# Where the rotary tables and the splits of weight units 4 and 5 stand in the first stage of a decoder trunk

## The chip, the cores and the metric

The kernel runs on one core of a Trainium2 chip. The metric is device time in microseconds of one execution, the median of several runs; lower is better. One further execution was profiled, and all lines of the profile are from it.

## The reference

Two decoder layers over 256 tokens of width 1024, in float32. What matters here is the start of the first layer:

```python
cos, sin = rope_tables(positions)           # angles: position x inverse frequency
h = rmsnorm(x, attn_norm[l])
q, k, v = jnp.split(h @ w_qkv_a[l], 3, axis=-1)
q = partial_rope(heads(q, N_HEADS), cos, sin)   # the first 16 of each head's 64 dims
k = partial_rope(heads(k, N_HEADS), cos, sin)
o = moba_attention(to_bhsd(q), to_bhsd(k), to_bhsd(heads(v, N_HEADS)))
```

With 256 tokens and a block of 256, this attention is plain causal attention of 16 heads. Then follow its output projection, a gated feed-forward layer with a causal convolution, a second layer of sliding-window attention with shared keys and values and a second feed-forward layer, and a last norm.

## The kernel before, in words

**Units and splits.** All weights are packed into units of 128 x 2048 values. Unit i is fetched by SyncE into the raw tile `wr` of that number (three buffers in rotation, so unit i + 3 waits for the last read of unit i). Each value is then split into a high part `wh`, rounded to TensorE's fp32r type, and a low part `wl`, the rest; the activations are split the same way, and a product is three matmuls (high x high, high x low, low x high), accumulated in PSUM. `hi_part` (L163) makes the high part on ScalarE, `lo_part` (L166) the low part on VectorE. `wh` and `wl` have four buffers each. A unit is split in quarters of 512 columns or halves of 1024.

**The first stage.** Units 0 and 1 are the first half of V's weights, which arrive chunk by chunk together with x (`first_parts`, `v_first`); units 2 and 3 are the weights of Q and K of head group 0, units 4 and 5 of group 1, 6 and 7 of group 2, 8 and 9 the second half of V, 10 and 11 of group 3. TensorE computes the first V half, then `qk_group(0)`: for each 128 rows of weights, three matmuls into each of two accumulators (K's and Q's, column half 0), then column half 1 of K's and of Q's. `rotate_f` (L418) reads such an accumulator on VectorE in four instructions (a shuffle, two products with the tables, a sum), ScalarE makes the high part (L432), VectorE the low part (L437), and GpSimd copies K's parts into the block-diagonal tile `kd` (L952). `scores` then multiplies Q and K of a group, and the softmax of its four heads runs on VectorE (L514, L535, L542) and ScalarE (L524, L540), while TensorE works on the next groups from a generator of filling work; `attention` gets a lead of 8000 (ns of counted TensorE work) between the end of group 0 and the first scores. After the softmax TensorE turns the probabilities (L555) and multiplies them by V (L578).

**The row norm and the tables.** The norm's factor per token is not applied to x but later, to the accumulated products. `square` (ScalarE, L301) sums the squares of a row block's halves, `rstd_of` takes two small VectorE instructions (L308, L309) and a GpSimd power (L310). V is scaled by it in `v_out` (L840). For Q and K the factor is folded into the rotary tables: `tables` makes sine and cosine (VectorE L917, GpSimd L918, ScalarE L919, GpSimd L922 and L923), `new_tables` spreads them over 64 dims on GpSimd (L390 to L394), scales them per row block on ScalarE (L400), has TensorE turn them (L406, four transposes) and ScalarE copy the result out (L411). `rotate_f` cannot run before that.

**What sets the order.** In this first stage PE, ScalarE, VectorE and SyncE run in the order in which the code issues (`manual`); GpSimd's and everything behind the stage is ordered by a scheduler. The order of issuing comes from deferred chains: `chain` puts a step off to a time on a counted clock, `tick` advances that clock by the work of each matmul and runs what is due, `require` forces a step. `first_norm` is put off to 3000 and `tables_a` to 3010 on that clock; `used(0)` and `used(1)` put the splits of units 4 and 5 off, four quarters each, with a fetch of unit i + 3 at the end of unit i.

## Time and profile before

| | us |
|---|---|
| median of 3 runs | 569.88 |
| lowest, highest | 569.54, 570.95 |
| the profiled execution | 569.15 |
| its span, first to last instruction | 567.4 |
| mean granted TensorE clock | 0.991 |

A timeline row gives start and length in microseconds, engine, line, operation, the tiles written and read, their shapes and the count of instructions merged; in brackets stands the idle time of the engine just before it and what ended it. A row of waits gives the total, the number of times and the longest. A windows row gives a stretch, its length, then each engine's busy time (PE, PEld, VectorE, ScalarE, GpSimd) with its number of instructions, the granted clock (PEclk), the share of the DMA engines and GB/s. An issues row ends in the microseconds from issue to landing. DVE is VectorE, ACT ScalarE, POOL GpSimd, SPq SyncE's queue. Times count from the start of the span.

### The profile page before, as it was taken

To read this page: it belongs to the slowest core of one execution; us is meant where nothing else is said; L and a number is where in the kernel's file an instruction comes from. 1 tells how busy PE (TensorE), PEld (TensorE's weight loads), DVE (VectorE), ACT (ScalarE), POOL (GpSimd) and SP (SyncE) were. 2 spreads that over 40 slices of the span, in tenths; PEclk is the share of its full clock that TensorE was granted. 3 is DMA by queue.
4 is the path that set the end of the run, shared out by engine and by line. 5 is a ranking of instruction groups with operands and counts; after the bars stand their busy time and mean duration, and the time that the engine had idled before them with its cause. 6 is when DMAs were issued, how large, how long until landed. Compare 5 with 4: busy or idle time off the path is not lost.

```text
span 567.4 us, 10530 instructions
## 1 busy us (share of the span) xinstructions
PE 550.1 (97%) x4022; PEld 512.6 (90%) x4022; DVE 437.0 (77%) x928; ACT 379.0 (67%) x771; POOL 104.0 (18%) x130
## 2 busy tenths in 40 slices
PE   8789999999999999999999999999999999999995
PEld 7679989889999999988887988889999999998884
DVE  6589988788899888864449989878988888874414
ACT  6846887887567777753439788887666777763413
POOL 7221102002232233110000100001432233210003
PEclk9889999999999999999999999999999999999998
DMA  8834472533384666555561832333265566666301
GB/s 321 361 120 178 153 243 77 206 139 103 122 288 160 222 223 223 200 198 202 217 219 43 268 137 96 129 98 126 102 219 206 218 223 223 213 210 222 135 0 74
DMA packets 15312, 101.00 MB, mean 178 GB/s; under 512 B 1952, under 2 KB 2080, under 8 KB 3744
## 3 DMA queue, kind: packets, MB, share of 16 engines
q1 hardware_dynamic: 14976, 100.09, 49.6%
q8 instruction: 31, 0.51, 0.3%
q10 hardware_dynamic: 288, 0.26, 0.1%
q14 instruction: 17, 0.14, 0.1%
HBM read 99.30 MB, written 1.05 MB: 177 GB/s over the span
## 4 chain that ended last, share of the span: by engine, by line
PE 84%; DVE 7%; ACT 4%; DMA 2%; issue 1%; POOL 1%; SPq 0%; DVEq 0%; POOLq 0%; ACTq 0%
PE acc L628 9%; PE acc L629 9%; PE acc L633 9%; PE u L725 6%; PE u L724 6%; PE u L723 6%; PE t L725 6%; PE t L724 6%; PE t L723 6%; DVE wl L167 3%; PE acc L452 2%; PE acc L454 2%; PE acc L453 2%; PE acc L724 2%; PE acc L723 2%; PE acc L725 2%
## 5 line engine op out<-in xcount | busy, mean ns | idle before, releaser
L167 DVE TENSOR_TENSOR wl<-wr,wh 128x1024 fp32r<-128x1024 f32 (+1 forms) x208 | 222.6, 1087 | 64.8 <-ACT wh L164 63.5
L164 ACT ACTIVATE wh<-wr 128x1024 fp32r<-128x1024 f32 (+1 forms) x208 | 189.4, 944 | 63.3 <-PE acc L633 51.7
L767 POOL TENSOR_TENSOR m<-m,m 128x256 f32<-128x256 f32 x44 | 64.7, 1470 | 176.2 <-DVE m L762 111.1
L628 PE MATMUL acc<-wh,q 128*128 128x512 f32 x238 | 92.0, 386 | 0.0
L629 PE MATMUL acc<-wl,q 128*128 128x512 f32 x238 | 90.6, 380 | 0.0
L723 PE MATMUL u<-q,wh 128*128 128x256 f32 x320 | 88.4, 277 | 0.0
L724 PE MATMUL u<-q,wh 128*128 128x256 f32 x320 | 88.2, 276 | 0.0
L725 PE MATMUL u<-q,wl 128*128 128x256 f32 x320 | 88.0, 275 | 0.0
L725 PE MATMUL t<-q,wl 128*128 128x256 f32 x288 | 79.2, 275 | 0.0
L723 PE MATMUL t<-q,wh 128*128 128x256 f32 x288 | 79.2, 275 | 0.0
L724 PE MATMUL t<-q,wh 128*128 128x256 f32 x288 | 79.2, 275 | 0.0
L633 PE MATMUL acc<-wh,q 128*128 128x512 f32 x238 | 74.6, 379 | 0.0
L724 PEld LDWEIGHTS u<-q,wh 128*128 128x128 f32 x320 | 60.1, 188 | 0.0
L725 PEld LDWEIGHTS u<-q,wl 128*128 128x128 f32 x320 | 60.1, 188 | 0.0
L723 PEld LDWEIGHTS u<-q,wh 128*128 128x128 f32 x320 | 59.9, 188 | 0.0
L723 PEld LDWEIGHTS t<-q,wh 128*128 128x128 f32 x288 | 54.1, 188 | 0.0
L724 PEld LDWEIGHTS t<-q,wh 128*128 128x128 f32 x288 | 54.1, 188 | 0.0
L725 PEld LDWEIGHTS t<-q,wl 128*128 128x128 f32 x288 | 54.1, 188 | 0.0
L628 PEld LDWEIGHTS acc<-wh,q 128*128 128x128 f32 x238 | 45.0, 189 | 7.0 <-issue 0.9
L633 PEld LDWEIGHTS acc<-wh,q 128*128 128x128 f32 x238 | 45.0, 189 | 6.3
L629 PEld LDWEIGHTS acc<-wl,q 128*128 128x128 f32 x238 | 45.0, 189 | 5.9 <-issue 0.2
L771 ACT ACTIVATE q<-m 128x256 fp32r<-128x256 f32 x44 | 18.1, 416 | 40.0 <-POOL m L767 40.0
(187 smaller groups left out, 1129.4 us busy)
## 6 DMA issues: line engine op xcount, KB each, us to landing
wr<-in_w SPq DMA_DIRECT2D x90, 1024.0 KB, 4.8
first<-in_xw SPq DMA_DIRECT2D x5, 384.0 KB, 5.9
xr<-in_x SPq DMA_DIRECT2D x2, 512.0 KB, 8.2
first<-in_xw SPq DMA_DIRECT2D x1, 768.0 KB, 7.3
fin_t<-in_fin SPq DMA_DIRECT2D x1, 512.0 KB, 5.7
out<-ot SPq DMA_DIRECT2D x1, 512.0 KB, 2.6
first<-in_xw SPq DMA_DIRECT2D x1, 388.0 KB, 3.6
out<-m ACTq DMA_DIRECT2D x1, 256.0 KB, 2.1
```

Of the source, the lines that this page charges most:

```text
L164: nc.scalar.activation(wq[i][0][:, c], raws[i][:, c], AF.Copy)
L167: nc.vector.tensor_tensor(out=wq[i][1][:, c], in0=raws[i][:, c], in1=f(wq[i][0][:, c]), op=ALU.subtract)
L452: nc.tensor.matmul(om, wh, xh, start=(c == 0), stop=False)
L453: nc.tensor.matmul(om, wh, xl, start=False, stop=False)
L628: nc.tensor.matmul(pairs(o), ph[:, blk(b)], turns(hi[:, s_]), start=first, stop=False)
L629: nc.tensor.matmul(pairs(o), ph[:, blk(b)], turns(lo[:, s_]), start=False, stop=False)
L633: nc.tensor.matmul(pairs(o), pl[:, blk(b)], turns(hi[:, s_]), start=False, stop=end)
L723: nc.tensor.matmul(o, hi[:, s_], xh, start=(c == 0), stop=False)
L724: nc.tensor.matmul(o, hi[:, s_], xl, start=False, stop=False)
L725: nc.tensor.matmul(o, lo[:, s_], xh, start=False, stop=(c == KC - 1))
L767: nc.gpsimd.tensor_tensor(out=h, in0=gs, in1=t[1], op=ALU.mult)
L771: (3400.0, lambda: nc.scalar.activation(hi, h, AF.Copy)),
```

## The change

It does four things. The sine, its tables and their spreading are issued between the second and the third quarter of unit 3's splits. Unit 4 is split by VectorE alone: it makes the high part with a cast (`both_parts`) and the low part as before, and the squares and row statistics stand between its quarters; then the tables are scaled and V copied out. Unit 5's four quarters follow at once, on ScalarE and VectorE, with the fetches of units 7 and 8 beside them. The transposes of the tables are put off to 7700 on the counted clock, and the lead ahead of the first scores is 9000 instead of 8000. The deferred chains of units 4 and 5 are gone; later units start from a time of 8500.

```diff
     tab = [None]
+    TURN = 7700.0
-    def new_tables(rs_, key, *wait):
-        ex = mid().rearrange("p (b k e d) -> p b k e d", b=NB, k=2, e=2)
-        nc.gpsimd.memset(ex[:, :, 0, :, ROT:], 1.0)
-        nc.gpsimd.memset(ex[:, :, 1, :, ROT:], 0.0)
-        for k, t in enumerate((cs, sn)):
-            for e in range(2):
-                nc.gpsimd.tensor_copy(ex[:, :, k, e, :ROT], t)
+    def new_tables(rs_, key, between):
+        ex = tab[0]
         sc = mid().rearrange("p (b k f) -> p b k f", b=NB, k=2)
         new = quad(F32, "tab")[:, :2]
-        def scale():
-            for b in range(NB):
-                nc.scalar.activation(sc[:, b], ex[:, b].rearrange("p k e d -> p k (e d)"), AF.Copy, scale=rs_[b])
+        for b in range(NB):
+            nc.scalar.activation(sc[:, b], ex[:, b].rearrange("p k e d -> p k (e d)"), AF.Copy, scale=rs_[b])
+            between(b)
...
-        chain(key, *wait, (0.0, scale), (1200.0, turn))
+        chain(key, (TURN, turn))
...
-    for j in range(4):
-        part(3, slice(j * 512, (j + 1) * 512))
-    fetch(6)
-    nc.sync.dma_start(cp, cpk)
...
     def tables():
...
+        ex = mid().rearrange("p (b k e d) -> p b k e d", b=NB, k=2, e=2)
...
+        tab[0] = ex
+
+    for j in range(4):
+        part(3, slice(j * 512, (j + 1) * 512))
+        if j == 1:
+            tables()
+    fetch(6)
+    nc.sync.dma_start(cp, cpk)
...
     v_first(KC - 1)
-    def first_norm():
-        for b in range(NB):
-            for n in range(2):
-                square(b, n)
-            rs.append(rstd_of(b))
-        for b in range(NB):
-            v_out(b, 0, v_acc[b])
-    chain(("rs",), (3000.0, first_norm))
-    def tables_a():
-        tables()
-        new_tables(rs, ("rt",))
-    chain(("rt",), (3010.0, tables_a))
-    used(0)
-    used(1)
+    def quarter(k):
+        return slice(k * 512, (k + 1) * 512)
+    def both_parts(i, k):
+        nc.vector.tensor_copy(wq[i][0][:, quarter(k)], raws[i][:, quarter(k)])
+        lo_part(i, quarter(k))
+    weights(4)
+    weights(5)
+    for b in range(NB):
+        for n in range(2):
+            square(b, n)
+        both_parts(4, b)
+        rs.append(rstd_of(b))
+    new_tables(rs, ("rt",), lambda b: (v_out(b, 0, v_acc[b]), both_parts(4, 2 + b)))
+    fetch(7)
+    for k in range(4):
+        part(5, quarter(k))
+    fetch(8)
+    w_time[0] = 8500.0
...
-    attention(qk, ready_a, filler_a(), 8000.0, lambda g: (7000.0, 3500.0, 2000.0) if g < 3 else (4500.0, 2000.0, 1500.0), mask, lambda h: h, False)
+    attention(qk, ready_a, filler_a(), 9000.0, lambda g: (7000.0, 3500.0, 2000.0) if g < 3 else (4500.0, 2000.0, 1500.0), mask, lambda h: h, False)
```

In the rows of the order, `wh4_288` is the high part of unit 4, `wr4` its raw tile; numbers behind the underscore differ between the two programs. ScalarE, from unit 3 to the copy of the turned tables, before:

```order
L164 ACTIVATE wh3_253<-wr3_200 128x512 x4
L301 ACTIVATE m2_15_316,st_14_315<-xr0_92 128x512
L301 ACTIVATE m2_16_318,st_14_315<-xr0_92 128x512
L301 ACTIVATE m2_19_325,st_18_324<-xr1_93 128x512
L301 ACTIVATE m2_20_327,st_18_324<-xr1_93 128x512
L840 ACTIVATE v0_101<-acc_7_113,rstd_17_320 128x512
L840 ACTIVATE v1_102<-acc_8_114,rstd_21_329 128x512
L919 ACTIVATE rb_94<-rb_94 128x32
L400 ACTIVATE m2_23_349<-m2_22_342,rstd_17_320 128x256
L400 ACTIVATE m2_23_349<-m2_22_342,rstd_21_329 128x256
L164 ACTIVATE wh4_359<-wr4_238 128x512 x2
L411 ACTIVATE tab_24_350<-t_25_369 128x512
```

The same place on ScalarE now, where the sine is the instruction that writes `rb` and the tables' scaling the one that writes `m2_19`:

```order
L164 ACTIVATE wh3_253<-wr3_200 128x512 x2
L911 ACTIVATE rb_94<-rb_94 128x32
L164 ACTIVATE wh3_253<-wr3_200 128x512 x2
L301 ACTIVATE m2_12_293,st_11_292<-xr0_92 128x512
L301 ACTIVATE m2_13_295,st_11_292<-xr0_92 128x512
L301 ACTIVATE m2_16_304,st_15_303<-xr1_93 128x512
L301 ACTIVATE m2_17_306,st_15_303<-xr1_93 128x512
L395 ACTIVATE m2_19_314<-m2_10_268,rstd_14_299 128x256
L836 ACTIVATE v0_101<-acc_7_113,rstd_14_299 128x512
L395 ACTIVATE m2_19_314<-m2_10_268,rstd_18_310 128x256
L836 ACTIVATE v1_102<-acc_8_114,rstd_18_310 128x512
L164 ACTIVATE wh5_290<-wr5_251 128x512 x4
```

The sine has moved ahead of four squares and two V copies, the scaling stands ahead of each V copy, and unit 4 is gone from this engine.

VectorE from unit 3's splits to the first rotation's neighbourhood, before:

```order
L167 TENSOR_TENSOR wl3_254<-wr3_200,wh3_253 128x512 x4
L308 TENSOR_TENSOR st_14_315<-st_14_315 128x1
L309 TENSOR_SCALAR st_14_315<-st_14_315 128x1
L308 TENSOR_TENSOR st_18_324<-st_18_324 128x1
L309 TENSOR_SCALAR st_18_324<-st_18_324 128x1
L917 SCALAR_TENSOR_TENSOR rb_94<-rb_94 128x16
L167 TENSOR_TENSOR wl4_360<-wr4_238,wh4_359 128x512 x3
```

The same place on VectorE now, up to the second row block's statistics (two more casts and splits of unit 4 and the four splits of unit 5 follow):

```order
L167 TENSOR_TENSOR wl3_254<-wr3_200,wh3_253 128x512 x2
L909 SCALAR_TENSOR_TENSOR rb_94<-rb_94 128x16
L167 TENSOR_TENSOR wl3_254<-wr3_200,wh3_253 128x512 x2
L941 CAST wh4_288<-wr4_238 128x512
L167 TENSOR_TENSOR wl4_289<-wr4_238,wh4_288 128x512
L308 TENSOR_TENSOR st_11_292<-st_11_292 128x1
L309 TENSOR_SCALAR st_11_292<-st_11_292 128x1
L941 CAST wh4_288<-wr4_238 128x512
L167 TENSOR_TENSOR wl4_289<-wr4_238,wh4_288 128x512
L308 TENSOR_TENSOR st_15_303<-st_15_303 128x1
L309 TENSOR_SCALAR st_15_303<-st_15_303 128x1
```

The row statistics stand behind casts of unit 4 now, where they stood directly behind unit 3.

VectorE around unit 7 and the first mask steps of the softmax (`ISA`), before, from unit 7's first half on (the four instructions that write `m2_35` and `m2_34` are a rotation):

```order
L167 TENSOR_TENSOR wl7_551<-wr7_423,wh7_550 128x1024
L426 STREAM_SHUFFLE m2_35_527<-acc_32_453 128x512
L427 TENSOR_TENSOR m2_34_526<-acc_32_453,tab_24_350 128x512
L428 TENSOR_TENSOR m2_35_527<-m2_35_527,tab_24_350 128x512
L429 TENSOR_TENSOR m2_34_526<-m2_34_526,m2_35_527 128x512
L167 TENSOR_TENSOR wl6_493<-wr6_263,wh6_492 128x1024
L167 TENSOR_TENSOR wl7_551<-wr7_423,wh7_550 128x1024
L514 ISA m3_39_594,hst_41_596<-acc_36_569,mask_274 128x128
```

The same place on VectorE now, from that rotation to unit 7's second half:

```order
L422 STREAM_SHUFFLE m2_35_530<-acc_32_459 128x512
L423 TENSOR_TENSOR m2_34_529<-acc_32_459,tab_20_315 128x512
L424 TENSOR_TENSOR m2_35_530<-m2_35_530,tab_20_315 128x512
L425 TENSOR_TENSOR m2_34_529<-m2_34_529,m2_35_530 128x512
L167 TENSOR_TENSOR wl7_542<-wr7_324,wh7_541 128x1024
L510 ISA m3_39_615,hst_41_617<-acc_36_588,mask_336 128x128
L510 ISA hst_41_617 128x1
L433 TENSOR_TENSOR q_31_458<-m2_34_529,q_30_457 128x512
L510 ISA m3_40_616,hst_41_617<-acc_36_588,mask_336 128x128
L510 ISA hst_41_617 128x1
L167 TENSOR_TENSOR wl8_613<-wr8_334,wh8_612 128x1024
L167 TENSOR_TENSOR wl7_542<-wr7_324,wh7_541 128x1024
```

Unit 6 is done ahead of the rotation, and between the two halves of unit 7 stand two mask steps, a low part and half of unit 8. On TensorE 87 matmuls of units 4 and 5 stand ahead of the first scores, where 75 stood, and the four transposes of the tables stand behind 33 more matmuls of units 2 and 3.

## The prediction

> **What bounds the kernel now.** I read the page's head first, then the list of waits of TensorE.

> ```profile
> span 567.4 us, 10530 instructions
> PE 550.1 (97%) x4022; PEld 512.6 (90%) x4022; DVE 437.0 (77%) x928; ACT 379.0 (67%) x771; POOL 104.0 (18%) x130
> PE t L406 <- ACT m L400: 4.1, 1, 4.1
> PE acc L454 <- DVE wl L167: 2.5, 1, 2.5
> ```

> TensorE is the bound. Its two longest waits, the only ones above 2 us, lie in the stretch that the change rewrites. Its timeline there, with two windows of granted clock (column PEclk, third from the end):

> ```profile
> 21.00 0.28 PE L454 MATMUL acc<-q,wl 128*128 128x256 f32 x1
> 25.42 1.12 PE L406 MATMUL t<-ident,m 128*128 128x128 f32 x4 [4.14 <-ACT m L400]
> 26.18 0.56 PE L452 MATMUL acc<-q,wh 128*128 128x256 f32 x1
> 28.74 0.28 PE L452 MATMUL acc<-q,wh 128*128 128x256 f32 x1
> 30.89 0.28 PE L453 MATMUL acc<-q,wh 128*128 128x256 f32 x1
> 38.83 0.58 PE L454 MATMUL acc<-q,wl 128*128 128x256 f32 x1 [2.54 <-DVE wl L167]
> 42.32 0.29 PE L452 MATMUL acc<-q,wh 128*128 128x256 f32 x1
> 27.00:28.00 1.00, 1.00 (x6) 1.00 (x6) 0.77 (x3) 1.00 (x3) 0.00 (x0) 0.50 0.32 127
> 40.00:42.00 2.00, 2.00 (x12) 2.00 (x11) 2.00 (x3) 1.68 (x2) 1.90 (x2) 0.50 0.71 201
> ```

> Each wait is paid twice: the gap itself, then about 3.4 us of work at clock 0.50. At full clock a 256-column matmul starts every 0.113 us (19 steps from 28.74 to 30.89); I use 0.114.

> **What goes.** Gap one, 4.14. After it, 4 transposes and 12 matmuls fill 25.42 to 28.74, 3.32 us; at 0.114 a step they would take about 1.8, so 1.5 goes with it. Gap two, 2.54. After it 16 matmuls fill 38.83 to 42.32, 3.49 us against 1.82, so 1.67 goes. Together 9.85 us. What the chip gives of this depends on what is late next; I walk the new order with old durations.

> **Sine among unit 3's quarters.** The splits and the sine's steps as they stand now:

> ```profile
> 15.04 5.00 DVE L167 TENSOR_TENSOR wl<-wr,wh 128x512 fp32r<-128x512 f32 x8 [0.35 <-ACT wh L164]
> 16.88 2.20 ACT L164 ACTIVATE wh<-wr 128x512 fp32r<-128x512 f32 x4 [0.30 <-DMA wr<-in_w]
> 21.82 0.17 DVE L917 SCALAR_TENSOR_TENSOR rb<-rb 128x16 f32<-128x16 f32 x1
> 22.63 0.20 POOL L918 TENSOR_SCALAR rb<-rb 128x16 f32<-128x16 f32 x1
> 23.16 0.22 ACT L919 ACTIVATE rb<-rb 128x32 f32<-128x32 f32 x1
> ```

> VectorE's eight quarters step by 0.60, so the second of unit 3 ends at 20.04 - 1.2 = 18.84. Then 0.17, 0.20 and 0.22 in turn, with some 0.1 of handing over each time: the sine is done at 19.5, and unit 3's last two ScalarE quarters (0.52 a step), which queue behind it, end near 20.05 and 20.6. Their VectorE halves end near 20.8 and 21.4 instead of 20.04. TensorE wants the third quarter's low part at 20.66 (three steps before 21.00): a wait of 0.2 (0.1 to 0.3). The third square then starts 1.5 later than before, which nobody on the path waits for yet. GpSimd's table copies run beside this and are read only at 25, so they cost nothing; if GpSimd were 5 us slower, the moved transposes would wait for them.

> **Unit 4 on VectorE, the row statistics behind it.** Unit 4's issue and landing, a split by cast, and the statistics:

> ```profile
> 12.72 0.33 SPq L161 DMA_DIRECT2D wr<-in_w  x1
> wr<-in_w SPq DMA_DIRECT2D x1, 1024.0 KB, 9.4
> 4.38 0.43 DVE L879 CAST wh<-first 128x512 fp32r<-128x512 f32 x1 [3.33 <-DMA first<-in_xw]
> 20.33 0.16 DVE L308 TENSOR_TENSOR st<-st 128x1 f32<-128x1 f32 x1 [0.29 <-ACT m L301]
> 21.43 0.67 ACT L840 ACTIVATE v<-acc,rstd 128x512 f32<-128x512 f32 x1
> 24.86 0.91 ACT L400 ACTIVATE m<-m,rstd 128x256 f32<-128x256 f32 x2 [1.48 <-POOL m L394]
> ```

> This is the added wait: VectorE's first cast waits for unit 4, which lands at 12.72 + 9.4 = 22.1, and both row blocks' statistics are queued behind casts on it. A quarter costs 0.47 (cast and hand-over) + 0.60 = 1.07, block 0's two small statistics about 0.27, so block 1's start at 22.15 + 2 x 1.07 + 0.27 = 24.55. From such a start to the first ScalarE instruction that uses the result pass 1.1 us (20.33 to 21.43, through GpSimd), and a scaled table takes 0.46 (half of 0.91): block 1's is there by about 26.1. TensorE no longer stops ahead of unit 3's last chunk; it goes on from 21.3 through 6 + 24 + 3 matmuls, 3.75 us, and reaches the moved transposes at 25.05. Two of the four use block 0 and run; the other two wait until 26.2. So of gap one 0.95 stays (0.5 to 1.5). From 26.4, 21 + 87 matmuls lead to the first scores: 26.4 + 108 x 0.114 = 38.7.

> On SyncE the fetch of unit 6 waits for unit 3's last split, 21.4 instead of 20.04; those of units 7 and 8 follow units 4's and 5's last reads, near 27 and 30. At the long landing of 9.4 they are there by 31, 36.5 and 39.5, while ScalarE, walked the same way, wants them at 33, 36.5 and 38.5: no cost, with unit 8 the tight one. ScalarE loses unit 4's four quarters, 2.2 us, which is why unit 5 follows at once.

> **What is late next: unit 7's second half.** In the new order VectorE has, from unit 5 to that half, four quarters, three rotations, two 512-column low parts, one more low part, two narrow mask steps and five halves of 1024.

> ```profile
> 30.98 0.74 DVE L426 STREAM_SHUFFLE m<-acc 128x512 f32<-128x512 f32 x1
> 33.53 2.09 DVE L167 TENSOR_TENSOR wl<-wr,wh 128x512 fp32r<-128x512 f32 x3
> 39.29 0.68 DVE L437 TENSOR_TENSOR q<-m,q 128x512 fp32r<-128x512 f32 x1
> 39.89 1.22 DVE L167 TENSOR_TENSOR wl<-wr,wh 128x1024 fp32r<-128x1024 f32 x1
> 41.03 0.88 DVE L437 TENSOR_TENSOR q<-m,q 128x512 fp32r<-128x512 f32 x1
> 40.04 2.14 POOL L952 CAST kd<-q 64x256 fp32r<-64x256 f32 x2 [4.16 <-DVE q L437]
> 47.71 1.42 DVE L167 TENSOR_TENSOR wl<-wr,wh 128x1024 fp32r<-128x1024 f32 x1
> 46.95 0.13 PE acc L494
> 48.57 0.32 PE acc L452
> 49.05 0.28 DVE L514 CUSTOM_DVE_ANT_0 m<-acc,mask 128x128 f32<-128x128 f32 x1
> ```

> A rotation takes 2.55 (30.98 to 33.53), a low part 0.60 (39.29 to 39.89), a half 1.14 (39.89 to 41.03), a mask step at most 0.28 (49.05). Unit 5's first quarter follows ScalarE's scale, v copy (0.58) and quarter (0.62) after 26.1, so VectorE takes it at 27.35. Then 4 x 0.60 + 3 x 2.55 + 3 x 0.60 + 2 x 0.28 + 4 x 1.14 + 1.22 for the last = 18.2: the half is there at 45.55. Rows at 41.03 (0.88 against 0.68) and 47.71 (1.42 against 1.22) show what GpSimd's casts beside VectorE cost, 0.2 each; up to three of them lie here, so 45.2 (the mask steps shorter, hand-overs nothing) to 46.2, and I take 45.65.

> [...]

> TensorE has 1.62 of scores (46.95 to 48.57), then 9 left of the 21 matmuls of unit 5 (12 more now stand ahead of the scores), 12 of unit 6 and 8 of unit 7: 38.7 + 1.62 + 29 x 0.114 = 43.65. So it waits 2.0 us (1.5 to 2.6) for a half that today is there at 49.13, when TensorE, with 21 + 12 + 8 steps behind 48.57, wants it at 53.2. A lead of 4 us becomes a lag of 2, since VectorE works without pause and now splits half of unit 8 ahead of it.

> **The first softmax.**

> ```profile
> 52.10 0.49 ACT L540 ACTIVATE m<-m,hst 128x256 f32<-128x256 f32 x1
> 56.29 0.66 PE u L555 x6
> 50.27 1.04 ACT L164 ACTIVATE wh<-wr 128x1024 fp32r<-128x1024 f32 x1
> 336.21 0.55 PE L555 MATMUL u<-ident,m 128*128 128x128 f32 x3 [1.25 <-ACT m L561]
> 336.00:338.00 2.00, 1.79 (x16) 1.79 (x17) 1.60 (x10) 1.36 (x4) 0.00 (x0) 1.00 0.42 90
> 63.45 0.22 PE acc L324
> ```

> Today the first head's probabilities are ready 3.7 us before TensorE turns them (52.10 + 0.49 against 56.29). VectorE loses the 6 us computed above against TensorE, and 2.0 of them are waited off at unit 7; 3.7 - 4.0 leaves 0.3 missing. In the new ScalarE order three halves of splits, 1.04 each, stand between the first head's exponentials and its scaled probabilities, today one; part of the two more lies beside VectorE's own lateness, so one of them on top, 1.3, is the high guess, and I take 1.1 (0 to 2). That the later groups have room is an estimate from the list of waits, which has no VectorE split in it behind 38.83.

> **Sum.** -9.85 + 0.2 + 0.95 + 2.0 + 1.1 = -5.6. The profiled execution took 569.15 us (span 567.4 and 1.75 around it), which gives 563.55; the median of the runs is 569.88, 0.73 above it, so 564.3. What follows after the first attention stands in the same order and only moves. The first L324 should come near 57.5 instead of 63.45.

> **Rivals.** *The clock falls again in the new wait.* A wait of 1.25 left it at 1.00 (336.00:338.00), one of 2.54 halved it; 2.0 lies between. If it falls, 1.67 is paid, but VectorE catches up meanwhile and the softmax wait mostly goes: net 1.2, 565.5. Chance 0.17. [...]

> *VectorE keeps up.* If splits, casts and hand-overs run a little faster than laid end to end, waits at unit 7 and softmax shrink to about half a microsecond: 561.7. Chance 0.13. Against it: the lag is the sum of plain durations.

> *The old gap stays.* The change puts statistics behind unit 4's landing. Were it 3.2 us later, the first gap would be 4.1 again with its 1.5 of slow clock, and 0.9 of gain is left: 569. Nothing ahead of unit 4 in SyncE's queue moves, so 0.06.

> *Slower: VectorE becomes the bound.* If each of the four head groups of this attention waits on VectorE as the first does, but 2.9 us each, 11.6 replaces 9.85: with the two small waits, about 572.8. It decides from 2.2 us a group, where nothing is gained, and from 2.6 where it is slower by more than 1.7. Against it: TensorE waits for no VectorE split behind 38.83 today, and each of its own waits gives VectorE that time back. Chance 0.03.

> **How the numbers follow.** The forecast as told has 0.61. Its own range, with all its unknown terms at one end (2.1 or 6.4 of waits against the 4.25 taken), is 562.1 to 566.4; the range that holds 8 in 10 takes in the first two rivals, 561.5 to 566.8. A measurement of this kernel tells about 0.3%, 1.7 us, from no change. Faster by more: forecast, clock rival and VectorE keeping up, 0.91. Within: 0.06. Slower: 0.03.

> **What would show it.** Right: the list of waits has the moved transposes at about 1 us, a matmul of unit 7 waiting on a VectorE split about 2 us near 44, and softmax transposes about 1; scores begin near 38.7; no window at 25 to 30 has a clock of 0.50. Wrong: the transposes still wait 3 us or more (unit 4's landing), clock 0.50 near 46 (first rival), no wait near 44 (second), or VectorE waits in every head group up to 110 (slower).

## The result, and the profile after

The changed kernel took 563.96 us (median of 4 runs, 563.05 to 564.46), the kernel before 570.41 beside it (4 runs, 569.54 to 571.02): a ratio of 0.9886, 95% interval 0.9866 to 0.9907. The profiled execution took 563.05, the lowest of the four, where that of before took 569.15. The forecast was 564.3, with a range of 561.5 to 566.8.

The head of the page and the longest waits of TensorE in the changed kernel (two waits that were there before too, 1.3 at L551 for L557 and 1.1 at L258, are left out):

```profile
span 561.2 us, 10529 instructions
```

```profile
PE acc L450 <- DVE wl L167: 2.0, 1, 2.0
...
PE t L402 <- ACT m L395: 0.7, 1, 0.7
PE u L551 <- ACT m L536: 0.4, 2, 0.2
```

The waits of 4.1 and 2.5 are gone; in their place stand 0.7 at the moved transposes and 2.0 at a low part. TensorE's timeline shows where: the moved transposes, the first scores, unit 7's second half, and the first transpose behind the attention.

```profile
26.18 0.44 PE L402 MATMUL t<-ident,m 128*128 128x128 f32 x2 [0.67 <-ACT m L395]
...
38.74 0.29 PE L490 MATMUL acc<-kd,q 128*128 128x256 f32 x1
...
46.08 0.39 PE L450 MATMUL acc<-q,wl 128*128 128x256 f32 x1 [2.03 <-DVE wl L167]
...
112.89 0.60 PE L271 MATMUL t<-ident,xr 128*128 128x128 f32 x4
```

In the kernel before, the last of these stood here:

```profile
119.18 0.60 PE L271 MATMUL t<-ident,xr 128*128 128x128 f32 x4
```

So 6.29 of the gain is there by the end of the first attention, and the span is shorter by 6.2: nothing behind that point took part. The windows of the changed kernel show the granted clock (third column from the end) behind both new waits:

```profile
27.00:28.00 1.00, 1.00 (x11) 1.00 (x11) 0.74 (x2) 1.00 (x3) 0.00 (x0) 1.00 0.44 101
46.00:48.00 2.00, 1.92 (x16) 1.93 (x17) 2.00 (x9) 1.75 (x6) 0.29 (x1) 1.00 0.43 78
```

The first of them had six matmuls at clock 0.50 before and has eleven at 1.00 now. Behind the new wait at 46 the clock stayed at 1.00 in this execution. VectorE works without a pause all through that wait; what it does in it and ahead of it stands in its timeline (the first cast of unit 4, unit 5's four quarters, a low part with the half behind it, a later low part, and the two halves that end with the one waited for), with GpSimd's:

```profile
22.03 0.43 DVE L941 CAST wh<-wr 128x512 fp32r<-128x512 f32 x1 [0.72 <-DMA wr<-in_w]
...
27.26 2.50 DVE L167 TENSOR_TENSOR wl<-wr,wh 128x512 fp32r<-128x512 f32 x4 [0.29 <-ACT wh L164]
...
36.61 0.88 DVE L433 TENSOR_TENSOR q<-m,q 128x512 fp32r<-128x512 f32 x1
37.41 1.42 DVE L167 TENSOR_TENSOR wl<-wr,wh 128x1024 fp32r<-128x1024 f32 x1
...
42.66 0.69 DVE L433 TENSOR_TENSOR q<-m,q 128x512 fp32r<-128x512 f32 x1
...
43.47 2.56 DVE L167 TENSOR_TENSOR wl<-wr,wh 128x1024 fp32r<-128x1024 f32 x2
```

```profile
35.62 2.14 POOL L962 CAST kd<-q 64x256 fp32r<-64x256 f32 x2 [1.21 <-DVE q L433]
...
42.12 4.16 POOL L962 CAST kd<-q 64x256 fp32r<-64x256 f32 x4 [4.37 <-ACT q L428]
```

The last of VectorE's rows ends at 46.03, and TensorE goes on at 46.08.

### The profile page after: what moved, and what is told of

Read it like the earlier page. It is cut to its first block, busy times and chain, and to the rows that moved or that the text cites. A ratio compares the mean times of both kernels' runs of the same rounds, so it can differ in the third digit from the quotient of the medians.

```text
span 561.2 us, 10529 instructions
## 1 busy us (share of the span) xinstructions
PE 548.0 (98%) x4022; PEld 510.9 (91%) x4022; DVE 439.1 (78%) x932; ACT 377.0 (67%) x767; POOL 107.3 (19%) x130
## 3 DMA queue, kind: packets, MB, share of 16 engines
HBM read 99.30 MB, written 1.05 MB: 179 GB/s over the span
## 4 chain that ended last, share of the span: by engine, by line
PE 81%; DVE 9%; ACT 4%; DMA 3%; issue 2%; POOL 0%; SPq 0%; DVEq 0%; POOLq 0%; ACTq 0%
PE acc L624 9%; PE acc L625 9%; PE acc L629 9%; PE u L721 6%; PE u L719 6%; PE u L720 6%; PE t L721 6%; PE t L719 6%; PE t L720 6%; DVE wl L167 4%; PE acc L720 2%; PE acc L719 2%; PE acc L721 2%; PE t L574 2%; DMA wr<-in_w 2%
## 5 line engine op out<-in xcount | busy, mean ns | idle before, releaser
L167 DVE TENSOR_TENSOR wl<-wr,wh 128x1024 fp32r<-128x1024 f32 (+1 forms) x208 | 223.4, 1090 | 59.6 <-ACT wh L164 59.0
L164 ACT ACTIVATE wh<-wr 128x1024 fp32r<-128x1024 f32 (+1 forms) x204 | 187.4, 951 | 62.6 <-PE acc L629 49.0
L767 ACT ACTIVATE q<-m 128x256 fp32r<-128x256 f32 x44 | 18.1, 416 | 38.5 <-POOL m L763 38.5
## 6 DMA issues: line engine op xcount, KB each, us to landing
wr<-in_w SPq DMA_DIRECT2D x90, 1024.0 KB, 4.8
```

The costliest lines, as they stand in the source:

```text
L164: nc.scalar.activation(wq[i][0][:, c], raws[i][:, c], AF.Copy)
L167: nc.vector.tensor_tensor(out=wq[i][1][:, c], in0=raws[i][:, c], in1=f(wq[i][0][:, c]), op=ALU.subtract)
L767: (3400.0, lambda: nc.scalar.activation(hi, h, AF.Copy)),
```

## The experiments

Ratios are to the kernel before, run beside each; the profiled execution of a run is one of those that its median is taken from. "The theory" and "the rival" are those of the quoted expectation. The first eight runs take the new waits apart one by one; the last four are about the clock, which behaved in a way that no size of wait explained.

### Unit 8's splits later

```diff
-        steps = [(w_time[0] - clock[0], first)]
+        steps = [(w_time[0] - clock[0] + (2500.0 if i == 8 else 0.0), first)]
```

> The changed kernel with unit 8's splits put off by 2500 on the counted clock, so that on VectorE no half of unit 8 stands ahead of unit 7's second half any more (one narrow mask step moves there instead). Theory (from unit 4's landing to that half VectorE works without pause, and its chain of work sets when TensorE goes on): the half is ready 1.14 - 0.21 = 0.9 us earlier, the wait near 44 falls from 2.03 to 1.1, and the time falls by 0.9 to about 563.0. Rival (VectorE is late for the softmax anyway): the 0.9 comes back as a longer wait of the softmax transposes, 0.2 now and 1.1 then, and the time stays at 564.

Measured: 563.46 (562.56 to 564.45), ratio 0.9873 (0.985 to 0.9897); profiled execution 564.45. Its waits of TensorE, the window ahead of a fall of the clock with the one behind it, and rows of TensorE (the first scores) and VectorE (unit 5's quarters, unit 7's second half):

```profile
PE t L402 <- ACT m L395: 1.8, 2, 1.0
...
PE u L551 <- DVE m L538: 1.1, 1, 1.1
```

```profile
24.30:27.70 3.40, 1.69 (x14) 1.25 (x12) 3.26 (x10) 1.54 (x4) 1.34 (x2) 1.00 0.77 302
27.80:31.10 3.30, 3.29 (x16) 3.30 (x17) 2.98 (x6) 3.09 (x6) 0.00 (x0) 0.50 0.43 132
```

```profile
41.90 0.29 PE L490 MATMUL acc<-kd,q 128*128 128x256 f32 x1
```

```profile
28.88 2.50 DVE L167 TENSOR_TENSOR wl<-wr,wh 128x512 fp32r<-128x512 f32 x4 [0.28 <-ACT wh L164]
...
45.30 1.46 DVE L167 TENSOR_TENSOR wl<-wr,wh 128x1024 fp32r<-128x1024 f32 x1
```

The wait at unit 7 is gone, but in this execution that alone shows nothing of unit 8: TensorE came to the scores 3.2 later (41.90 instead of 38.74), and the half itself ended at 46.76, later than the 46.03 of the changed kernel. What the edit did shows in the length of VectorE's chain. From unit 5's first quarter to the end of that half it took 17.88, where the changed kernel took 18.77 (27.26 to 46.03): 0.89 less, as the theory told. A wait of 1.1 stands in the first softmax, for VectorE again, as the rival told. The median is 0.5 below the changed kernel's, and their intervals overlap: half a hit.

The lateness isn't the edit's. Unit 4's first cast began at 23.66 in this execution instead of 22.03, though nothing ahead of it had changed; the transposes then waited twice, 1.8 together, and the clock fell to 0.50 for 3.4 us. Of its four executions two had a mean granted clock of 0.993 and 0.995 and took 564.17 and 564.45; the other two, at 0.996 and 0.999, took 562.56 and 562.75, below all of the changed kernel's.

### The transposes early again

```diff
-    TURN = 7700.0
+    TURN = 4200.0
```

> The changed kernel with the transposes of the tables at their old place, ahead of unit 3's last chunk (4200 in place of 7700). Theory (VectorE's chain sets the end of this stretch, TensorE only part of it): TensorE waits about 4.5 us near 21 to 26 and works at half clock behind it, but the wait of 2.0 at unit 7 goes, since VectorE's chain is later by only 1.2; the time rises by 3.3, to about 567.3. Rival (each gap counts by itself): gap 3.8 more and slow clock 1.5, the wait at unit 7 stays; the time rises by 5.3, to about 569.3.

Measured: 566.98 (566.59 to 568.23), ratio 0.9944 (0.9924 to 0.9964). Its waits, and two windows:

```profile
PE t L402 <- ACT m L395: 5.3, 2, 4.7
```

```profile
20.20:23.60 3.40, 1.10 (x8) 0.71 (x6) 1.35 (x3) 2.72 (x9) 1.52 (x5) 1.00 0.90 328
23.70:27.00 3.30, 0.69 (x2) 0.29 (x2) 3.06 (x10) 1.10 (x3) 1.54 (x3) 0.50 0.91 375
```

The theory holds: the old gap is back with its slow clock, here for two stretches of 3.4 us (23.62 to 30.45), and 3.0 of the gain is lost, as the sum of gap and later relief had it (567.3). Moving the transposes is a condition of the gain.

### The transposes moved in the kernel before

```diff
-        chain(key, *wait, (0.0, scale), (1200.0, turn))
+        chain(key, *wait, (0.0, scale), (4900.0, turn))
```

> The kernel before with one part of the change alone: only the transposes of the tables are later, behind 33 more matmuls. Theory (removing one wait of TensorE uncovers VectorE's chain): the first gap shrinks to about 0.8 and its slow clock goes, 4.8 in all, but the splits of unit 4's last quarter and of unit 5 still stand behind the rotations on VectorE, so that TensorE waits near 30 to 36 for 4.9 in place of 2.5; the third quarter of unit 5 is ready at 36.2 instead of 38.8, and the time falls by 2.6, to about 567.8. Rival (gaps add up): the time falls by 4.8, to 565.6.

Measured: 566.95 (566.24 to 567.5), ratio 0.9939 (0.992 to 0.9958). Its waits, and two windows:

```profile
PE acc L454 <- DVE wl L167: 4.2, 3, 2.5
```

```profile
29.10:32.50 3.40, 1.89 (x14) 1.51 (x14) 3.37 (x7) 2.48 (x6) 0.71 (x1) 1.00 0.01 2
32.50:35.90 3.40, 1.06 (x6) 0.65 (x6) 3.37 (x7) 0.94 (x2) 0.77 (x2) 1.00 0.85 308
```

The time lies 0.85 below the theory and 1.35 above the rival, nearer to the theory. This one edit gives 3.5 of the 6.45: gap one goes, and TensorE runs into the splits of units 4 and 5 instead (1.51, 0.18 and 2.52). The other 3.0 come only with the rest of the change, which has those splits ready earlier. Behind the first wait the clock stayed at 1.00 (second row); behind the last, from 36.0 on, it was 0.50 for 3.4 us.

### ScalarE makes unit 4's high parts

```diff
     def both_parts(i, k):
-        nc.vector.tensor_copy(wq[i][0][:, quarter(k)], raws[i][:, quarter(k)])
-        lo_part(i, quarter(k))
+        part(i, quarter(k))
```

> The changed kernel with unit 4's high parts on ScalarE again, at the same places of the order; VectorE loses four casts, 1.9 us. The scheduler then puts unit 7's second half ahead of unit 8's first on VectorE. Theory (ScalarE, with the squares, the scaling and the V copies, becomes the feeder): unit 5's first quarter comes about 1.0 later, near 28.3, the transposes wait 1.2 instead of 0.67, and unit 7, helped by 1.35 by the order alone, waits about 1.3; the time falls by 0.2 to 0.3. Rival (only VectorE's load counts): the chain is 1.9 earlier, with the order 3.2, the wait at unit 7 is gone, and the time falls by 2.0, to about 562.0.

Measured: 564.08 (563.55 to 564.67), ratio 0.9894 (0.9879 to 0.9908). The wait at the transposes grew to 1.0, that at unit 7 shrank to 1.2, and softmax transposes took 1.2 waiting for VectorE. The waits together are 0.9 more in this execution; the median is 0.1 more than the changed kernel's, where the theory told 0.2 to 0.3 less and the rival 2.0 less. The rival is out, and which engine makes unit 4's high parts is not what the gain hangs on. That it hangs on their being made at once is left over from these runs, not shown by one of its own.

### The sine behind unit 3

```diff
-        if j == 1:
+        if j == 3:
             tables()
```

> The changed kernel with the sine behind all four quarters of unit 3 and not among them. Theory (unit 4's landing at 22.0 sets what follows, so the sine's place buys nothing): the tables are spread by 23.2, still ahead of the first row statistic at 24.3, the first cast still starts at 22.0; the time stays at 564.0 within 0.3. Rival (the sine's place is a part of the gain): squares and statistics come 1.2 later and the time rises by 1.2, to 565.2.

Measured: 563.69 (563.04 to 564.89), ratio 0.9889 (0.9873 to 0.9905): the same, as the theory had it. The sine's place between the quarters buys nothing here. But this profiled execution took 564.89, and shows this (timeline, then a window):

```profile
45.84 0.39 PE L450 MATMUL acc<-q,wl 128*128 128x256 f32 x1 [2.04 <-DVE wl L167]
```

```profile
46.90:50.20 3.30, 3.30 (x18) 3.30 (x17) 3.30 (x15) 3.30 (x9) 0.00 (x0) 0.50 0.76 298
```

The wait of the changed kernel, in the same place and of the same size (2.04 against 2.03), and here the clock falls behind it. The prediction's first rival had come, in one execution and not in the other.

### The transposes later still

```diff
-    TURN = 7700.0
+    TURN = 9600.0
...
-        chain(key, (150.0, turn), (2600.0, high), (700.0, low))
+        chain(key, (1100.0 if key == ("qk", 0) and then is not None else 150.0, turn), (2600.0, high), (700.0, low))
```

> The changed kernel with the transposes of the tables behind nine more matmuls and the first rotation's issue later, so that TensorE does not wait for the tables. Theory (VectorE's chain sets the end of this stretch): the wait of 0.67 at the transposes goes, the wait of 2.03 at unit 7 grows by as much, the time stays at 564.0 within 0.3. Rival (waits of TensorE add up): the time falls by 0.7, to 563.3.

Measured: 563.37 (562.8 to 564.24), ratio 0.9879 (0.9862 to 0.9897). The time is nearer to the rival but doesn't tell the two apart. The waits say more; then the window of the longest:

```profile
PE acc L450 <- DVE wl L167: 1.9, 2, 1.6
...
PE acc L491 <- POOL kd L962: 0.9, 1, 0.9
```

```profile
43.40:46.80 3.40, 1.76 (x15) 1.57 (x14) 3.40 (x8) 3.15 (x9) 2.56 (x3) 1.00 0.00 0
46.80:50.20 3.40, 3.40 (x30) 3.17 (x28) 3.40 (x13) 3.40 (x9) 0.00 (x0) 1.00 0.86 308
```

The transposes no longer wait; in exchange the scores wait 0.9 for GpSimd's copies into `kd`. The wait moved from the one to the other, so the waits did not add up as the rival has it; but it did not move to unit 7 either, as the theory told: the wait there is 1.6 instead of 2.03.

### A lead of 8000

```diff
-    attention(qk, ready_a, filler_a(), 9000.0, ...
+    attention(qk, ready_a, filler_a(), 8000.0, ...
```

> The changed kernel with the lead ahead of the first scores back at 8000: 75 instead of 87 matmuls stand ahead of the scores. VectorE's order changes with it: both halves of unit 7 stand ahead of the mask steps and of unit 8. Theory (the order of VectorE's chain sets the wait at unit 7): scores wait about 0.4 for GpSimd's copies of K (there at 37.8), unit 7's second half is ready near 43.7, so that its wait goes; the softmax transposes wait 0.5 or so; the time falls by 1.2, to about 562.8. Rival (the longer lead is needed): the copies of K are waited for 1.4 and the softmax 1.5, the time rises by 0.9.

Measured: 565.05 (564.47 to 565.86), ratio 0.9908 (0.9889 to 0.9927). Here the theory fell, and the rival's size was right: the median is 1.1 above the changed kernel's, though the intervals overlap. TensorE's timeline, then its windows:

```profile
50.75 0.59 PE L551 MATMUL u<-ident,m 128*128 128x128 f32 x3 [1.80 <-DVE m L538]
```

```profile
47.80:51.20 3.40, 1.60 (x13) 1.39 (x13) 3.40 (x13) 3.40 (x12) 0.00 (x0) 1.00 0.00 0
51.30:54.60 3.30, 3.30 (x18) 3.30 (x17) 3.30 (x7) 3.30 (x6) 0.00 (x0) 0.50 0.44 134
```

With the scores twelve matmuls earlier the wait at unit 7 goes, but the softmax then waits for VectorE, 1.80 here and 0.17 at 47.65: the same amount in another place. The copies of K, which the rival had at 1.4, were waited for 0.2. Since VectorE is what is late, the order of TensorE's work can only choose where to wait. In this execution the clock fell behind the wait, and the mean granted clock of all four executions is 0.995, as low as this one's: it seems to have fallen in each of them, against one in four of the changed kernel's. That would explain the 1.1; traces of the other three, which could show it, were not kept.

### Four edits together

The tables' row statistics stand behind unit 4's first quarter, ScalarE makes the high parts of its last two, V's copies come later, and unit 8 is put off by 2500, by the line of the first experiment, which is left out here:

```diff
-        both_parts(4, b)
+    both_parts(4, 0)
+    for b in range(NB):
         rs.append(rstd_of(b))
-    new_tables(rs, ("rt",), lambda b: (v_out(b, 0, v_acc[b]), both_parts(4, 2 + b)))
+    both_parts(4, 1)
+    for k in (2, 3):
+        part(4, quarter(k))
     fetch(7)
+    new_tables(rs, ("rt",), lambda b: None)
     for k in range(4):
         part(5, quarter(k))
+        if k == 1:
+            v_out(0, 0, v_acc[0])
     fetch(8)
+    chain(("v1",), (9900.0, lambda: v_out(1, 0, v_acc[1])))
...
```

> The changed kernel with four edits that shorten VectorE's chain: both row statistics directly behind unit 4's first quarter, ScalarE makes the high parts of unit 4's last two quarters in its pause behind the squares, the V copies stand behind the tables' scaling and among or behind unit 5's quarters, and unit 8's splits are put off by 2500. Theory: the transposes wait 0.4 or less, unit 5's first quarter starts on VectorE at 26.5 instead of 27.26, unit 7's second half is ready near 44.3 instead of 46.0, and its wait falls from 2.03 to 1.0; the time falls by 1.7, to about 562.3. Rival (the softmax takes the wait over): the time stays within 0.5 of 564.0.

Measured: 563.05 (562.15 to 563.55), ratio 0.9873 (0.9859 to 0.9888), the lowest median of all; it isn't told apart from the changed kernel (0.9866 to 0.9907). Its waits:

```profile
PE t L402 <- ACT m L395: 1.1, 1, 1.1
...
PE acc L450 <- DVE wl L167: 0.7, 2, 0.5
PE u L551 <- DVE m L538: 0.7, 1, 0.7
```

Unit 4 was late in this execution as well (its first cast at 23.34), so the transposes still waited. In this execution the matmuls of 256 columns between 18 and 62 us show no stretch at half clock (steps of 0.21 in the runs that have one, of 0.113 here), and the mean granted clock was 0.996.

### Idle products in the gaps of the kernel before

```diff
         def turn():
+            warm_up(7)
             t = bank("t")
...
+                warm_up(6 if triple[0] == 39 else 0)
                 nc.tensor.matmul(om, wl, xh, start=False, stop=(c == KC - 1))
+                triple[0] += 1
```

> The kernel before, with seven idle products of ones (0.47 us each at full clock) queued on TensorE ahead of the waiting transposes (gap 4.14) and six ahead of the low part that waits 2.54. They change no wait and no result; they only keep TensorE busy in the two gaps. Theory: half speed is granted for stretches of 3.4 us after a stretch of 3.4 us in which TensorE idled for more than half. Then no window between 21 and 43 us shows a clock of 0.50. TensorE comes 1.5 us earlier to the second gap, which is set mostly by VectorE and grows, and leaves it 1.67 us faster: 570.4 - 1.7 = 568.7, and up to 567.2 where VectorE's split follows TensorE's earlier start. Rival: the clock falls for another reason than idle time on TensorE (what the other engines do): 0.50 shows at 25 and at 39 as before, time 570.4 or up to 0.5 more.

Measured: 570.26 (568.85 to 570.89), ratio 1.0 (0.9987 to 1.0012). TensorE's timeline, then its windows:

```profile
20.89 1.72 PE L258 MATMUL u<-ones 128*128 128x128 f32 x14
...
25.22 0.84 PE L407 MATMUL t<-ident,m 128*128 128x128 f32 x4 [2.61 <-ACT m L400]
...
37.38 0.58 PE L458 MATMUL acc<-q,wl 128*128 128x256 f32 x1 [2.53 <-DVE wl L167]
...
38.19 2.74 PE L258 MATMUL u<-ones 128*128 128x128 f32 x12
...
42.28 0.28 PE L455 MATMUL acc<-q,wh 128*128 128x256 f32 x1
```

```profile
23.70:27.10 3.40, 1.88 (x15) 1.68 (x16) 0.98 (x2) 2.44 (x6) 1.10 (x7) 1.00 0.91 378
33.90:37.30 3.40, 0.85 (x6) 0.45 (x4) 3.37 (x8) 0.94 (x3) 0.53 (x1) 1.00 0.72 289
37.40:40.70 3.30, 3.30 (x16) 3.30 (x16) 3.30 (x5) 2.83 (x3) 2.05 (x2) 0.50 0.56 141
```

As a measurement of time the run failed: the six products meant for gap two were put one step too late, behind it, where they took 2.74 at the slow clock. The expectation also had the length of a product wrong: 0.47 is about what one takes at clock 0.50 (2.74 for six), and at full clock it is 0.25 (1.72 for seven), so gap one was filled to less than half.

As a test of the clock it is the best of all. In gap one the products took 1.72, a wait of 2.61 stayed, and the clock did not fall; TensorE came to the end of gap two 1.45 earlier than before (37.38 against 38.83), which is the price the prediction gave the slow clock of gap one (1.5). Gap two, unfilled, was 2.53, shorter than that 2.61, and the clock fell. The total agrees: the 1.45 went to the six products behind gap two, and the matmul that stood at 42.32 before stands at 42.28. All this is one execution. Of the ten, six had a mean granted clock of 0.990 or 0.991, where this one had 0.993; a further stretch of 3.4 us at half speed would make that difference, and where it lay no kept trace shows. So the products kept the clock here, and it isn't shown that they do in every execution.

### Idle products in the changed kernel, and the changed kernel twice more

The edit is the second one above, with four products at a later count, `triple[0] == 70`; the two others are the changed kernel unaltered.

> The changed kernel with four idle products of ones (1.9 us together) ahead of the matmul of unit 7 that waits 2.03. Theory: the clock falls there in some executions of the changed kernel and not in others, by how the wait lies against stretches of 3.4 us, so the idle products take away the bad cases: clock 1.00 from 44 to 52 in this execution, no wait above 0.3 at unit 7, and a median 0.3 to 0.8 below the changed kernel's 563.96, about 563.4. Rival: the clock never falls behind that wait in the changed kernel, and the products only stand in the way: 564.0 to 564.3.

> The changed kernel once more, for one more profiled execution. Theory: the granted clock behind the 2.0 us wait at unit 7 depends on where the wait lies in a stretch of 3.4 us that runs on regardless of the kernel; it falls to 0.50 for 3.4 us in about 6 of 10 executions (wholly inside a stretch, or more than 1.7 of it in one), and the execution then takes about 1 us more, 564 to 564.5 instead of 563.0. Rival: the clock is a property of the kernel and stays at 1.00 in each execution: 563.0 to 563.5.

> The changed kernel a third time, one more profiled execution, with the same expectations: by the theory a clock of 0.50 for 3.4 us behind the wait at unit 7 in about 6 of 10 executions, with about 1 us more of time; by the rival never. With the first look (1.00 throughout) and the one beside this, the theory fails if all three stay at 1.00 with chance 0.06 only.

Measured: with the products 564.46 (563.52 to 564.65), ratio 0.9903 (0.9884 to 0.9922); the changed kernel again 564.80 and 563.30, one execution each. The products missed the wait here, too: they stand at 50.46, behind it, 1.05 long (told: 1.9), so what they would have saved wasn't measured. All three executions answer the question of the clock, though. First the one with the products (timeline, then windows), then the two others (timelines, and a window of the former):

```profile
46.01 0.39 PE L453 MATMUL acc<-q,wl 128*128 128x256 f32 x1 [2.05 <-DVE wl L167]
```

```profile
46.60:49.90 3.30, 3.30 (x18) 3.30 (x17) 3.30 (x14) 3.30 (x9) 0.00 (x0) 0.50 0.86 300
```

```profile
47.11 0.39 PE L450 MATMUL acc<-q,wl 128*128 128x256 f32 x1 [2.06 <-DVE wl L167]
```

```profile
48.20:51.60 3.40, 3.40 (x18) 3.40 (x18) 3.40 (x16) 3.40 (x9) 0.00 (x0) 0.50 0.76 289
```

```profile
46.32 0.39 PE L450 MATMUL acc<-q,wl 128*128 128x256 f32 x1 [2.04 <-DVE wl L167]
```

The wait is 2.03 to 2.06 in every one of five executions with this order; the clock fell behind it in three (with the sine moved, with the products, and in the changed kernel's second profile) and stayed at 1.00 in two. The rival, that the clock is a property of the kernel, is out.

### What decides the clock

The changed kernel has three profiles: the first beside the result, the second and the third in the section above. The stretches at 0.50 in the first stage are 3.4 us long in the traces here, or twice that (23.62 to 30.45 with the transposes early). In the trace of the kernel before, the granted clock falls at 25.13, rises at 28.55, falls at 38.79, rises at 42.20 and falls for the last time, behind TensorE's last work, at 564.44. The last two are 522.24 apart, or 153 x 3.4133, and the others 1, 3 and 1 times as much. In the changed kernel's first profile the clock falls once, at the end:

```profile
556.60:556.70 0.10, 0.00 (x0) 0.00 (x0) 0.10 (x1) 0.10 (x1) 0.00 (x0) 0.84 0.00 0
```

That is at 556.67; 150 of the steps of the kernel before, taken back from there, give 44.67 (an estimate, as no change of the clock shows it here), inside the wait from 44.05 to 46.08. It cuts the wait into 0.62 and 1.41, and in neither stretch does TensorE idle for more than half:

```profile
41.20:44.60 3.40, 2.84 (x25) 2.65 (x24) 3.40 (x8) 3.14 (x4) 2.36 (x3) 1.00 0.48 202
44.60:48.00 3.40, 1.92 (x16) 1.93 (x17) 3.40 (x10) 3.15 (x10) 1.63 (x2) 1.00 0.25 46
```

The falls behind this wait, read from the windows and the steps of the matmuls, came at 46.9 with the sine moved, at 46.5 with the products and at 48.2 in the second profile: 2.2, 1.9 and 3.5 (a step and 0.1) behind 44.67, so the steps don't begin at the same place in every execution. In each of the three the whole wait lies within the 3.4 us ahead of the fall.

Sorted by TensorE's busy time in a stretch of 3.4 (second number of the rows above): behind 0.85, 1.06, 1.10, 1.60 and 1.69 the next stretch ran at 0.50; behind 1.76, 1.88, 1.89 and 1.92 at 1.00. In these rows, rounded to 0.1 us, the border lies between 1.69 and 1.76, about half of 3.4. With the traces of the kernel before and of the changed kernel's first profile cut at steps of 3.4133 back from the last fall, 322 stretches from 10 us on, those with 0.00 (twice), 0.83 and 1.32 of busy time are followed by 0.50, and all others, with 2.00 or more, by 1.00. With unit 8 later it took two waits in one stretch, 0.95 and 0.86. Of the single waits, those of 2.03 to 2.06 were followed by 0.50 in three executions and by 1.00 in two, those of 2.52 to 2.54 by 0.50 all three times, and one of 2.61 by 1.00.

For a wait of 2.04 at a random place, 0.6 is the estimate from these numbers (wholly inside a stretch in 0.40, more than 1.7 of it on one side in another 0.20); three of five were seen. The executions without a kept trace can be counted, too. In the profiles with no fall in the first stage the mean granted clock was 0.996 or 0.997, in those with one 0.993 to 0.995. Of all 14 executions with this order (six of the changed kernel, four with the sine moved, four with the products), six had 0.995 or less and took 564.3 to 564.9, and eight had more and took 563.0 to 564.1. So executions with a fall, counted by this mean, took 1.1 more on average.

## Why the prediction was right, point by point

- **The two gaps and their slow clocks (9.85).** Gone, as the clock of 1.00 at 27 and the list of waits show. The price of a slow clock was shown apart for gap one, in one execution: 1.45 against the 1.5 worked out.
- **Unit 3's third quarter (0.2).** The matmul that needs it started at 20.77, some 0.1 late. With the sine moved away the time was the same.
- **Moved transposes (0.95).** 0.67: unit 4 landed at 21.9 instead of 22.1. That landing was taken as fixed, and it isn't: VectorE's first cast began at 21.8 to 22.3 in some executions of the changed kernel and its variants and at 23.1 to 23.7 in four others; in the second profile (23.08) the transposes waited 1.6. The third rival needed a landing 3.2 later, and up to 1.6 was seen.
- **Unit 7's second half (2.0).** The wait is 2.03, but both ends were later than told, so that the agreement is in part luck. The half was there at 46.03 (told: 45.65). TensorE's last matmul ahead of it starts at 43.77 and ends at 44.05, from where the row counts; the next was due at 43.88 (told: 43.65), and counted as the prediction does the lag is 2.15. VectorE is without pause through it, and with unit 8 put off its chain up to the half was shorter by 0.89, so it is the length of that chain that TensorE waits for. With GpSimd's casts beside them, the low part at 36.61 took 0.88, and the half at 37.41 and the one waited for (at 44.60) took 1.42, 0.2 each above the 0.68 and 1.22 that the prediction took for such rows alone. That is 0.6, where the prediction added 0.1, and covers the half's lateness. But the low part at 42.66 and the half at 43.47, beside casts as well, took 0.69 and 1.22, so not every such row was longer; of the 147 low parts and splits in this trace with no cast beside them, none took over 0.70 (512 columns) or 1.23 (1024).
- **The first softmax (1.1).** The mis-sized term: 0.4 in two waits for L536, of which 0.2 was there before. The likely reason is that the lateness was counted twice in part, since VectorE uses the 2.0 at unit 7 to catch up: in the five runs in which that wait is shorter or gone, softmax transposes wait for VectorE (L538) 0.3 with the transposes later still, 0.7 with the four edits, 1.1 with unit 8 later, 1.2 with ScalarE's high parts and 2.0 with the lead of 8000.
- **The sum.** Told -5.6, measured -6.1 in the profiled executions and -6.45 between the medians. The terms with what they measured (0.1 + 0.67 + 2.03 + 0.2) would give -6.85; of the 0.75 between, 0.2 is TensorE's later arrival at unit 7, and the rest is not assigned. So the softmax term was 0.9 too big, and 0.75 is missing elsewhere: that they offset each other, and the total came within 0.35 of the median, is luck. The first scores came at 38.74 (told: 38.7), the first L324 at 57.1 (57.5). The 0.73 between profile and median that the sum adds seems to belong to the kernel before alone: of its 27 executions beside the experiments, 16 had a mean clock of 0.989 and a span 1.1 longer than the other 11, which had 0.991 or 0.992 as the profiled one has. A third slow stretch would do that, and no kept trace shows it.
- **The rival with the clock (chance 0.17, net price 1.2).** It came in single executions, not in the median. Its price was right: 1.1 on average in the 14 executions above. In the traces, a fall put the end of the attention (the first L271) back by 1.5 against the first profile with the sine behind unit 3 (out of the wait 0.24 earlier, at L271 1.23 later) and by 0.75 in the second profile (1.03 later, then 1.78); in the third, without a fall, it was 0.24 later at both. What failed is the ground of its chance: the prediction asked whether 2.0 lies nearer to 1.25 or to 2.54, as if the length decided, and waits of 2.03 to 2.06 were followed by 0.50 in three executions and by 1.00 in two. Of the four executions behind 563.96 one had the mean clock of those with a fall (0.994, 564.46). The two in the middle, 563.87 and 564.05, have the highest clock of all, 0.999, so what set them 0.8 and 1.0 above the first profile is not the clock. For the one it is time outside the span, which is 561.0 against the first profile's 561.2; for the other it stays open.
- **VectorE as the bound.** It didn't come: behind 46 TensorE waits for no VectorE split, and for VectorE at all only 0.3 (at L574) and 0.2 (at L365), both there before.

## What to carry to other kernels

When a gap on the bounding engine is removed, walk the new order with old durations up to the next thing that arrives late. Here the walk found it (a half of a split, some 2 us), and the experiments could move that wait to the scores, the softmax or the transposes, but hardly shorten it while VectorE had no pause. Price a gap on TensorE by the idle time that falls into one stretch of 3.4 us. In these runs idle time of up to 1.64 in one (1.76 busy) cost itself alone; from 1.71 on (1.69 busy) the next stretch ran at 0.50, which cost 1.45 where it was shown apart and 1.1 on average at unit 7. With a gap between half a stretch and a whole one it went both ways (2.53 halved the clock here, 2.61 didn't). So get the idle time in such a stretch, of all its waits together, below 1.6 rather than shave what stays above it, and read more than one execution before a clock of 1.00 is called safe.
